# Two edits to an fp32 encoder kernel: low parts of early FFN weights by adding DMAs, and the order of the first norm

## The chip, the cores and the metric

The kernel runs on one core of a Trainium2 chip. The metric is the device time of one execution in microseconds (us); lower is better. The core's engines are named as in the profile: PE multiplies matrices (PEld is its weight load), DVE, ACT and POOL work on vectors, SP issues DMAs. POOL and ACT can issue DMAs as well. Each engine works through its own list of instructions in order, and waits at an instruction until what it needs is there.

## The reference

Two layers of an encoder over 512 tokens of width 1024, in float32. What matters here:

```python
for l in range(DEPTH):                      # DEPTH = 2
    h = rms_norm(x, g_pre_mix[l])
    z = h @ w_in[l]                         # q, k, v, conv parts, two gates
    ...                                     # windowed attention and a short convolution
    mix = (sigmoid(ga) * y_attn + sigmoid(gb) * y_conv) @ w_out[l]
    x = x + rms_norm(mix, g_post_mix[l])
    h = rms_norm(x, g_pre_ffn[l])
    f = (silu(h @ w_gate[l]) * (h @ w_up[l])) @ w_down[l]   # d_ff = 2816
    x = x + rms_norm(f, g_post_ffn[l])
```

`rms_norm(x, g)` is x / sqrt(mean(x²) + 1e-6) * g per token.

## The kernel before

**Split products.** Every float32 operand is held as two parts in a short matmul type: the high part `h` is a cast by ACT (L130 for weights, L212 for activations), the low part `lo` is raw − h, a subtraction on DVE (L131, L213). A product is then three matmuls (`mm3`, L181 to L183). There is a second way to make the low part, `split_by_dma` (L133 to L137): ACT casts (L135), ACT writes the cast's source with its sign turned into the place of `lo` (L136), and a DMA that POOL issues adds the source to it (L137), which leaves what the rounding of −src lost. As the lines stand:

```python
nc.scalar.copy(h, src)
nc.scalar.activation(lo, src, AF.Copy, scale=-1.0)
nc.gpsimd.dma_start(out=lo.bitcast(F32), in_=src, accum_op=ALU.add)
```

Weights come as 512 KB tiles: `raw` (3 buffers) or `u` (`unit`); split halves lie in `hl` tiles (8 buffers), 256 KB a part.

**FFN pairs.** The 22 gate/up pairs of a layer are computed by a scheme with seven products instead of eight (class `Pair`), numbered 1 to 7; (0,6) below means product 6 of pair 0. Products 2, 1 and 4 take a raw block of weights as it stands, products 5, 6, 3 and 7 take sums of blocks, made by DVE (L438). `need` loads, `prep` splits, `product` multiplies; `run_pairs` walks over a fixed list `seq`, and ahead of product n it loads for the next 10 products, and splits for the next 5. Where a product is in the pair's `by_dma`, its split is done up to 10 products ahead, by `split_by_dma`. The two gates of the mixer are pairs of the same class (`Gates`), with `by_dma = (4,)`; the FFN's pairs have none. `seq` begins with products 2 and 1 of the first five pairs (`EARLY`), then (0,5), (1,5), (0,6) and so on.

**The right-hand operands** of the FFN (class `Rights`) are sums of blocks of the normed activations. `turn(t)` transposes one token tile of 128 tokens on PE (L372) and makes what can be made from it; `sums(2)`, `sums(3)` make the rest once tiles 2 and 3 are there.

**The tail of w_out.** `down` multiplies by w_out; its last five k are kept and done tile by tile, so that the four token tiles end one after the other. Ahead of that, `ahead()` issues the loads of the first FFN weights and splits products 2 and 1 of pairs 0 to 2 (six splits). For each token tile, `post_norm` takes two square sums on ACT (L234), forms v on DVE, r on POOL (L228), and scales; `pre_norm` does the same once more for the FFN's norm. `turn(0)` stands after half of tile 2, `turn(1)` after half of tile 3; `turn(2)` and `turn(3)` among the first FFN products.

**The first norm** (layer 0, L608 and on) is written in a fixed order for all engines: loads, square sum, scaling, split of the first weights, transposes, products.

The rest is put in order by a scheduler, engine by engine, when the kernel is built.

Of the kernel before, what the change touches and what calls it, by code (L numbers as in the profile page):

```python
# [16 lines left out]
P = 128  # L17
D = 1024
# [10 lines left out]
FT = DFF // P  # L29
EPS = 1e-6  # L30
AHEAD = 5
LEAD = 12
NEG = -1e30
THETA = 500000.0
# [33 lines left out]
def encoder(ctx: ExitStack, tc: tile.TileContext, a, out):  # L68
    nc = tc.nc
# [9 lines left out]
    def in_order(*engines):  # L79
        return tc.manual_schedule(engines=set(engines))  # L80
# [3 lines left out]
    def nm(s):  # L84
        names[s] = names.get(s, -1) + 1
        return f"{s}_{names[s]}"

    def bank():
        return pp.tile([P, 512], F32, tag="bank", name=nm("bank"))
# [4 lines left out]
    def t4(shape, dtype=F32):  # L94
        return sp.tile(shape, dtype, tag="t4", bufs=6, name=nm("t4"))

    def t2(shape, dtype=F32):
        return sp.tile(shape, dtype, tag="t2", bufs=6, name=nm("t2"))

    def small(n, s="sm"):  # L100
        return sp.tile([P, n], F32, tag=s, bufs=4, name=nm(s))


    ident = cp.tile([P, P], F32, name="ident")
# [10 lines left out]
    def load_constants():  # L115
        nc.sync.dma_start(tab, a["tab"])
        nc.sync.dma_start(sink, a["attn_sink"].rearrange("l h -> (l h)").partition_broadcast(P))
        nc.sync.dma_start(cw_rows, a["conv_w"].rearrange("l j (c p) -> (l j c) p", p=P))
# [23 lines left out]
    def load_cols(w, c0, n, k0=0):  # L142

        raw = raw_tile()
        k = 1024 // n
        nc.sync.dma_start(
            raw.rearrange("p (k c) -> p k c", k=k),
            w[k0 * P : (k0 + k) * P, c0 : c0 + n].rearrange("(k p) c -> p k c", p=P),
        )
        return raw  # L150
# [4 lines left out]
    def split_cols(raw, n):  # L155

        tiles = []
        for hf in range(2):
            hl = hl_tile()
            split_w(raw[:, hf * 512 : hf * 512 + 512], hl[:, 0], hl[:, 1])  # L160
            tiles.append(hl.rearrange("p a (k c) -> p a k c", c=n))
        per = 512 // n
        return lambda part, k: tiles[k // per][:, part, k % per]

    def w_cols(w, c0):
        return split_cols(load_cols(w, c0, P), P)
# [53 lines left out]
    def rstd(ss):  # L220

        v = small(1, "v")
        nc.vector.tensor_scalar(v, ss, EPS, None, op0=ALU.add)
        return inv_sqrt(v)

    def inv_sqrt(v):
        r = small(1, "r")
        nc.gpsimd.tensor_tensor(out=r, in0=v, in1=half, op=ALU.pow)  # L228
        return r

    def square_sum(src, n):
        junk = t2([P, n], BF16)
        s = small(1, "ss")
        nc.scalar.activation(junk, src, AF.Square, scale=1.0 / 32.0, accum_out=s)  # L234
        return s

    def scale_rows(x, r, g):
        nc.vector.scalar_tensor_tensor(x, x, r, g, op0=ALU.mult, op1=ALU.mult)
# [5 lines left out]
    def turn(t, xs, hT):  # L244

        ts = slice(t * P, (t + 1) * P)
        for hf in range(2):
            pt = bank()
            for j in range(4):
                nc.tensor.transpose(  # L250
                    pt[:, j * P : (j + 1) * P], xs[:, (4 * hf + j) * P : (4 * hf + j + 1) * P], ident
                )
            ks = slice(4 * hf, 4 * hf + 4)
            split_to(hT[:, 0, ks, ts], hT[:, 1, ks, ts], pt.rearrange("p (k c) -> p k c", k=4))
# [247 lines left out]
    EARLY = 5  # L502
    READY = 3

    def orders(n, early):

        after = {1: 2, 6: 1, 7: 6, 4: 7, 3: 5}
        seq, at, opened = [], {}, 0

        def free(i, p):  # L510
            before = after.get(p)
            if before is None:
                return True
            if (i, before) not in at:
                return False
            return p == 1 or len(seq) - at[i, before] >= 3

        for i in range(early):
            seq += [(i, 2), (i, 1)]
            at[i, 2], at[i, 1] = len(seq) - 2, len(seq) - 1  # L520
        for i in range(2):
            at[i, 5] = len(seq)
            seq.append((i, 5))
        opened = early
        while len(seq) < 7 * n:
            left = [i for i in range(opened) if (i, 4) not in at]
            pick = next(
                ((i, p) for i in left for p in (5, 6, 3, 7, 4) if (i, p) not in at and free(i, p) and (p != 4 or (i, 3) in at)), None
            )
            if opened < n and (len(left) < 2 or pick is None):  # L530
                for p in (2, 1):
                    at[opened, p] = len(seq)
                    seq.append((opened, p))
                opened += 1
                continue
            if pick is None:
                pick = next((i, p) for i in left for p in (5, 6, 3, 7, 4) if (i, p) not in at)
            at[pick] = len(seq)
            seq.append(pick)
        return seq  # L540

    def run_pairs(pairs, seq, before=lambda n: None):
        for n, (i, p) in enumerate(seq):
            before(n)
            for j, q in seq[n : n + 2 * AHEAD]:
                pairs[j].need(q)
                if q in pairs[j].by_dma:
                    pairs[j].prep(q)
            for j, q in seq[n : n + AHEAD]:
                pairs[j].prep(q)  # L550
            pairs[i].product(p)
# [3 lines left out]
    g = t4([P, D])  # L555
    normed = [t4([P, D]) for _ in range(NT)]
    xsrc = a["x"]

    seq, gate_seq = orders(FT, EARLY), orders(KT, 2)

    for l in range(DEPTH):
# [44 lines left out]

        if l == 0:
            with in_order(E.PE, E.Activation, E.DVE, E.Pool, E.SP):  # L608
                nc.scalar.dma_start(g, a["g_pre_mix"][0].partition_broadcast(P))
                raws = []  # L610
                for t in range(NT):
                    nc.sync.dma_start(normed[t], a["x"][t * P : (t + 1) * P, :])
                    if t < 3:
                        raws.append(load_cols(w_in, *((V0, KV * HD, t * KT // 2) if t < 2 else (K0, P))))
                scale_rows(normed[0], rstd(square_sum(normed[0], D)), g)
                hv = [split_cols(raws[0], KV * HD)]
                r1 = rstd(square_sum(normed[1], D))
                turn(0, normed[0], hT)
                raws.append(load_cols(w_in, K0 + P, P))
                load_constants()  # L620
                scale_rows(normed[1], r1, g)
                hv.append(split_cols(raws[1], KV * HD))
                value_product(0, range(KT // 2))
                r2 = rstd(square_sum(normed[2], D))
                turn(1, normed[1], hT)
                value_product(0, range(KT // 2, KT))
                scale_rows(normed[2], r2, g)
                hk = [split_cols(raws[2], P)]
                value_product(1)
                value_split(0)  # L630
                scale_rows(normed[3], rstd(square_sum(normed[3], D)), g)
                hk.append(split_cols(raws[3], P))
                ka = [bank(), bank()]
                gemm_half(ka[:1], hk[:1], xs, 0)
                turn(2, normed[2], hT)
                value_split(1)
                gemm_half(ka[1:], hk[1:], xs, 0)
                turn(3, normed[3], hT)
                value_product(2)
                value_product(3)  # L640
                value_split(2)
                value_split(3)
            taps()
        else:
            hv = [split_cols(load_cols(w_in, V0, KV * HD, i * KT // 2), KV * HD) for i in range(2)]
            hk = [w_cols(w_in, K0 + i * P) for i in range(2)]
            value_tile(0)
            value_tile(1)
            turn(2, normed[2], hT)
            ka = [bank(), bank()]  # L650
            gemm_half(ka[:1], hk[:1], xs, 0)
            value_tile(2)
            turn(3, normed[3], hT)
            gemm_half(ka[1:], hk[1:], xs, 0)
            value_tile(3)
# [173 lines left out]
        total, done = (KT - 2 + 4 * KT) * KT, 0  # L829
        for _ in range(LEAD):  # L830
            next(steps)
        total -= LEAD
        for i, piece in enumerate(pieces):
# [74 lines left out]
        pairs = []  # L908
        for f in range(FT):
            pairs.append(Gated(r, a["w_gate"][l], f * P, a["w_up"][l], f * P))  # L910
            pairs[f].f = f

        def ahead():
            for i in range(READY):
# [31 lines left out]
        normed = [None] * NT  # L946
# [53 lines left out]
```

## Time and profile before

| | |
|---|---|
| time, median of 3 runs | 1663.45 us (1663.43 to 1664.44) |
| profiled execution | 1662.62 us, of it 1660.8 us in the profile's span |
| granted clock of PE, mean | 0.998 |
| stages of layer 0 (us of the span) | first norm 0 to 16; tail of w_out about 447 to 484; FFN start about 484 to 520 |
| FFN start of layer 1 | about 1305 to 1344 |
| adding DMAs in all | 16, from 360.8 to 1243.5 us |

The instructions of one line are a group; a row of the timeline has the start, the duration, the engine, the line, what was written from what, and in square brackets how long the engine had been idle and what ended that. A row of the waits has the total, the number and the longest. "q0 software_dynamic" is the queue of the DMAs that POOL issues, "q1 hardware_dynamic" that of SP and ACT. Lines are those of this kernel; the changed kernel's are 1 to 11 higher (1 higher up to L543).

### The profile page before, as it was taken

Reading aid. Unit: us, or ns where it says so; the run is one execution under the profiler, and the core shown is the slowest. Engines: PE = TensorE matmul, PEld = TensorE weight load, DVE = VectorE, ACT = ScalarE, POOL = GpSimd, SP = SyncE. Lnnn points to the kernel's source line nnn. Section 1 sums busy time; section 2 is a strip of 40 time slices with the busy share of each in tenths; the row PEclk is TensorE's granted clock in tenths of the full one; section 3 lists DMA queues with packets and bytes.
Section 4 is the critical chain, followed back from the end, with each engine's and each line's share of the span. In section 5 each row is a group of like instructions: output and inputs, shape, how many; then the busy total and the mean of one; then the engine's idle time right before and its main releaser. Section 6 shows DMA issues by size and latency. Waiting matters only on the chain.

```text
span 1660.8 us, 26449 instructions
## 1 busy us (share of the span) xinstructions
PE 1636.2 (99%) x10033; PEld 1470.2 (89%) x10033; DVE 1237.5 (75%) x2398; ACT 929.5 (56%) x1958; POOL 86.2 (5%) x130
## 2 busy tenths in 40 slices
PE   7999999999999999999999999999999999999998
PEld 7888888889989999988898888888998899999886
DVE  6988876749779988854469788756696898888442
ACT  5666666547656555543346676564575565556331
POOL 0000000000011100000000000000010011001000
PEclk9999999999999999999999999999999999999999
DMA  6322222345652333343413222223457243343332
GB/s 203 95 77 77 64 83 70 89 115 127 183 160 77 102 102 105 116 136 134 148 61 102 76 77 77 77 77 97 101 156 204 92 112 94 104 112 121 108 114 76
DMA packets 249248, 178.63 MB, mean 108 GB/s; under 512 B 5744, under 2 KB 233120, under 8 KB 249120
## 3 DMA queue, kind: packets, MB, share of 16 engines
q1 hardware_dynamic: 246096, 171.18, 35.1%
q0 software_dynamic: 2304, 4.20, 1.6%
q8 instruction: 78, 1.28, 0.3%
q10 hardware_dynamic: 720, 1.57, 0.3%
q14 instruction: 50, 0.41, 0.1%
HBM read 164.34 MB, written 8.39 MB: 104 GB/s over the span
## 4 chain that ended last, share of the span: by engine, by line
PE 96%; DVE 2%; DMA 1%; ACT 1%; issue 0%; POOL 0%; POOLq 0%; DVEq 0%; SPq 0%; ACTq 0%
PE bank L182 30%; PE bank L183 29%; PE bank L181 29%; PE bank L690 2%; PE bank L737 2%; PE bank L724 2%; PE bank L250 0%; DVE u L213 0%; DMA u<-in_w_up_dram 0%; DVE h L213 0%; DMA t<-in_x_dram 0%; ACT t L234 0%; DVE t L438 0%; DVE hl L131 0%; PE bank L372 0%
## 5 line engine op out<-in xcount | busy, mean ns | idle before, releaser
L181 PE MATMUL bank<-h,hl 128*128 128x256 f32 (+1 forms) x1536 | 493.7, 321 | 1.4 <-DVE h L213 1.4
L182 PE MATMUL bank<-h,hl 128*128 128x256 f32 (+1 forms) x1536 | 490.4, 319 | 0.4 <-DVE hl L131 0.4
L183 PE MATMUL bank<-h,hl 128*128 128x256 f32 (+1 forms) x1536 | 490.1, 319 | 0.0
L131 DVE TENSOR_TENSOR hl<-raw,hl 128x512 fp32r<-128x512 f32 x396 | 269.9, 692 | 167.6 <-ACT hl L130 166.2
L130 ACT CAST hl<-raw 128x512 fp32r<-128x512 f32 x396 | 241.8, 620 | 258.8 <-PE bank L183 216.7
L183 PEld LDWEIGHTS bank<-h,hl 128*128 128x128 f32 x1536 | 292.7, 191 | 20.8
L181 PEld LDWEIGHTS bank<-h,hl 128*128 128x128 f32 x1536 | 292.9, 191 | 19.9 <-DVE h L213 2.2
L181 PE MATMUL bank<-u,hl 128*128 128x256 f32 (+1 forms) x976 | 305.6, 313 | 4.1 <-DVE u L213 3.4
L182 PEld LDWEIGHTS bank<-h,hl 128*128 128x128 f32 x1536 | 292.9, 191 | 18.1 <-DVE hl L131 0.6
L182 PE MATMUL bank<-u,hl 128*128 128x256 f32 (+1 forms) x976 | 304.7, 312 | 2.9 <-ACT u L212 1.8
L183 PE MATMUL bank<-u,hl 128*128 128x256 f32 (+1 forms) x976 | 304.1, 312 | 0.0
L181 PEld LDWEIGHTS bank<-u,hl 128*128 128x128 f32 x976 | 186.6, 191 | 15.3 <-DVE u L213 3.8
L182 PEld LDWEIGHTS bank<-u,hl 128*128 128x128 f32 x976 | 186.8, 191 | 13.4 <-ACT u L212 2.2
L183 PEld LDWEIGHTS bank<-u,hl 128*128 128x128 f32 x976 | 186.8, 191 | 10.2
L131 DVE TENSOR_TENSOR hl<-t,hl 128x512 fp32r<-128x512 f32 x240 | 176.9, 745 | 22.5 <-ACT hl L130 19.9
L130 ACT CAST hl<-t 128x512 fp32r<-128x512 f32 x240 | 147.6, 621 | 72.4 <-DVE t L438 47.0
L182 PE MATMUL bank<-hl,u 128*128 128x512 f32 x304 | 118.3, 389 | 0.0
L181 PE MATMUL bank<-hl,u 128*128 128x512 f32 x304 | 118.3, 389 | 0.0
L183 PE MATMUL bank<-hl,u 128*128 128x512 f32 x304 | 118.3, 389 | 0.0
L710 ACT ACTIVATE t<-t,neg 128x256 f32<-128x256 f32 (+1 forms) x128 | 70.4, 552 | 21.1 <-DVE neg L705 20.8
L438 DVE TENSOR_TENSOR t<-t,raw 128x512 f32<-128x512 f32 x112 | 76.7, 696 | 1.2
L906 POOL TENSOR_TENSOR u<-t 128x256 f32<-128x256 f32 x44 | 51.8, 1178 | 398.0 <-DVE t L492 196.9
(137 smaller groups left out, 2275.1 us busy)
## 6 DMA issues: line engine op xcount, KB each, us to landing
raw<-in_w_in_dram SPq DMA_DIRECT2D x88, 512.0 KB, 3.9
u<-in_w_up_dram SPq DMA_DIRECT2D x44, 512.0 KB, 6.1
raw<-in_w_down_dram SPq DMA_DIRECT2D x44, 512.0 KB, 3.5
raw<-in_w_gate_dram SPq DMA_DIRECT2D x40, 512.0 KB, 3.9
raw<-in_w_conv_proj_dram SPq DMA_DIRECT2D x16, 512.0 KB, 4.3
raw<-in_w_attn_proj_dram SPq DMA_DIRECT2D x16, 512.0 KB, 4.3
u<-in_w_in_dram SPq DMA_DIRECT2D x16, 512.0 KB, 5.5
raw<-in_w_out_dram SPq DMA_DIRECT2D x16, 512.0 KB, 3.6
```

Source lines behind the costliest of these rows:

```text
L130: nc.scalar.copy(h, raw)
L131: eng.tensor_tensor(out=lo, in0=raw, in1=h.bitcast(F32), op=ALU.subtract)
L181: nc.tensor.matmul(acc, wh, xl, start=first, stop=False, skip_group_check=goes_on)
L182: nc.tensor.matmul(acc, wl, xh, start=False, stop=False, skip_group_check=goes_on)
L183: nc.tensor.matmul(acc, wh, xh, start=False, stop=last, skip_group_check=goes_on)
L438: add = lambda out, x, y: nc.vector.tensor_tensor(out=out, in0=x, in1=y, op=ALU.add)
L690: nc.tensor.matmul(s[:, :w], q, kk[g][:, 1 - part, lo_b * P : lo_b * P + w], start=part == 0, stop=part == 1)
L710: nc.scalar.activation(p, p, AF.Exp, bias=neg[:, i : i + 1], accum_out=den[:, i : i + 1])
L724: nc.tensor.transpose(pt[:, i * P : (i + 1) * P], p[:, n * P : (n + 1) * P], ident)
L737: nc.tensor.matmul(o, v, hl[:, 1 - part], start=n == 0 and part == 0, stop=kb == hi_b and part == 1)
L906: nc.gpsimd.tensor_tensor(out=out[:, TH:], in0=self.v[:, 1], in1=self.out0[:, TH:], op=ALU.mult)
```

## The change

1. **FFN.** Pairs 0 to 4 of both layers get `by_dma = (2, 1, 4)`: 15 low parts per layer, 30 in all, are made by an activation on ACT and an adding DMA instead of a subtraction on DVE.
2. **Look-ahead.** Splits by DMA are done up to 8 products ahead instead of 10 (`FAR`), for the mixer's gates too.
3. **First norm.** The load of `g_pre_mix` goes from ACT's queue to SP's, behind the first x tile. PE does 30 transposes of the identity, whose result nothing reads, at the start. The first token tile is scaled in two halves.

```diff
+FAR = 8
...
             for j, q in seq[n : n + 2 * AHEAD]:
                 pairs[j].need(q)
+            for j, q in seq[n : n + FAR]:
                 if q in pairs[j].by_dma:
                     pairs[j].prep(q)
...
-                nc.scalar.dma_start(g, a["g_pre_mix"][0].partition_broadcast(P))
+                idle = bank()
+                for _ in range(30):
+                    nc.tensor.transpose(idle[:, :P], ident, ident)
                 raws = []
                 for t in range(NT):
                     nc.sync.dma_start(normed[t], a["x"][t * P : (t + 1) * P, :])
+                    if t == 0:
+                        nc.sync.dma_start(g, a["g_pre_mix"][0].partition_broadcast(P))
...
-                scale_rows(normed[0], rstd(square_sum(normed[0], D)), g)
+                r0 = rstd(square_sum(normed[0], D))
+                for c in (slice(0, 512), slice(512, D)):
+                    scale_rows(normed[0][:, c], r0, g[:, c])
...
             pairs[f].f = f
+            if f < EARLY:
+                pairs[f].by_dma = (2, 1, 4)
```

What this does to the order on ACT, in the tail of w_out of layer 0. Before, after the last split of pair 2 (`raw_4725`), the two square sums of token tile 0 (`t_96`, `t_97`) and the one of its pre norm (`t_98`) follow each other:

```order
L130 CAST hl_4747<-raw_4725 128x512
L130 CAST hl_4750<-raw_4725 128x512
L234 ACTIVATE t_96_4788,ss_4789<-bank_4577 128x512
L234 ACTIVATE t_97_4795,ss_4796<-bank_4578 128x512
L234 ACTIVATE t_98_4805,ss_4806<-t_93_4783 128x1024
```

Now each split has a second row (L137), and the splits of pair 3 (`u_61` holds its gate weights) stand between the square sums:

```order
L136 CAST hl_4787<-raw_4757 128x512
L137 ACTIVATE hl_4787<-raw_4757 128x512
L235 ACTIVATE t_96_4826,ss_4827<-bank_4609 128x512
L136 CAST hl_5065<-u_61_4761 128x512
L137 ACTIVATE hl_5065<-u_61_4761 128x512
L136 CAST hl_5069<-u_61_4761 128x512
L137 ACTIVATE hl_5069<-u_61_4761 128x512
L235 ACTIVATE t_97_4833,ss_4834<-bank_4610 128x512
```

The second square sum `t_97` moved behind four operations on `u_61`.

On POOL, the last gate's adding DMA was followed at once by the r of the first post norm:

```order
L137 DMA hl_4401<-u_46_4307 128x512
L228 TENSOR_TENSOR r_4799<-v_4792,half 128x1
L228 TENSOR_TENSOR r_4810<-v_4808,half 128x1
```

Now the adding DMAs of pairs 0 to 3 stand ahead of it (the last four of eight are shown):

```order
L138 DMA hl_4783<-raw_4757 128x512
L138 DMA hl_4787<-raw_4757 128x512
L138 DMA hl_5065<-u_61_4761 128x512
L138 DMA hl_5069<-u_61_4761 128x512
L229 TENSOR_TENSOR r_4837<-v_4830,half 128x1
```

Eight DMAs moved in front of the first r; the two of pair 4 stand behind the eighth r.

On DVE, at the FFN start of layer 0, the subtractions of pairs 3 and 4 (`u_61`, `u_62`) stood behind the last pre norm's scaling (L242), among the pairs' outputs (L483):

```order
L242 SCALAR_TENSOR_TENSOR t_100_4998<-t_99_4997,r_5024,t_92_4575 128x1024
L131 TENSOR_TENSOR hl_5060<-t_108_5057,hl_5060 128x512
L483 TENSOR_TENSOR t_101_5063<-bank_5027,t_101_5063 128x256
L131 TENSOR_TENSOR hl_5078<-u_61_4729,hl_5078 128x512
L131 TENSOR_TENSOR hl_5094<-u_61_4729,hl_5094 128x512
L483 TENSOR_TENSOR t_102_5097<-bank_5081,t_102_5097 128x256
L131 TENSOR_TENSOR hl_5112<-u_62_4731,hl_5112 128x512
L131 TENSOR_TENSOR hl_5128<-u_62_4731,hl_5128 128x512
```

Now they are gone, and the sums for the right-hand operands (L400, L403, L214) follow sooner:

```order
L243 SCALAR_TENSOR_TENSOR t_100_5036<-t_99_5035,r_5062,t_92_4607 128x1024
L132 TENSOR_TENSOR hl_5106<-t_108_5103,hl_5106 128x512
L484 TENSOR_TENSOR t_101_5113<-bank_5073,t_101_5113 128x256
L439 TENSOR_TENSOR t_110_5201<-u_63_4765 128x512
L214 TENSOR_TENSOR h_4604<-u_66_5096,h_4604 128x4x128
L484 TENSOR_TENSOR t_102_5145<-bank_5132,t_102_5145 128x256
L132 TENSOR_TENSOR hl_5204<-t_110_5201,hl_5204 128x512
L400 SCALAR_TENSOR_TENSOR u_66_5096<-u_66_5096,u_64_4936 128x4x128
```

Four rows left this stretch, and L400 of the third token tile, which came after the fourth tile's first rows, moved up to here.

## The prediction

> **What bounds the kernel now.** I read the page first, then the waits of PE, then timelines where those waits lie.
>
> ```profile
> PE 1636.2 (99%) x10033; PEld 1470.2 (89%) x10033; DVE 1237.5 (75%) x2398; ACT 929.5 (56%) x1958; POOL 86.2 (5%) x130
> ...
> PE bank L250 <- DVE t L238: 9.5, 1, 9.5
> PE bank L181 <- DVE u L213: 3.4, 2, 1.7
> PE bank L182 <- ACT u L212: 1.8, 2, 0.9
> PE bank L182 <- DVE hl L131: 1.5, 4, 0.5
> ```
>
> PE is busy 99% of the span. The waits that it has (columns: total, times, longest; the four largest are shown, and sum to 16 us) lie at the start, 9.5, and where the FFN of each of the two layers begins. So the change can win only in these two places, and wherever it makes PE wait anew it costs one for one. The first norm:
>
> ```profile
> 6.12 1.06 ACT L234 ACTIVATE t<-t 128x1024 bf16<-128x1024 f32 x1 [3.65 <-DMA t<-in_x_dram]
> 8.12 1.29 DVE L238 SCALAR_TENSOR_TENSOR t<-t,r,t 128x1024 f32<-128x1024 f32 x1 [0.67 <-POOL r L228]
> 9.29 1.06 ACT L234 ACTIVATE t<-t 128x1024 bf16<-128x1024 f32 x1 [0.16 <-DMA t<-in_x_dram]
> 9.46 1.97 PE L250 MATMUL bank<-ident,t 128*128 128x128 f32 x8 [9.46 <-DVE t L238]
> 10.62 0.58 ACT L212 CAST h<-bank 128x512 fp32r<-128x512 f32 x1 [0.18 <-PE bank L250]
> 12.36 0.41 PE L183 MATMUL bank<-hl,h 128*128 128x256 f32 x1
> 12.57 0.41 PE L181 MATMUL bank<-hl,h 128*128 128x256 f32 x1
> 12.70 1.27 DVE L238 SCALAR_TENSOR_TENSOR t<-t,r,t 128x1024 f32<-128x1024 f32 x1
> ```
>
> The x tile sets the first square sum, and everything to the first product hangs on it. Matmuls follow each other here at 0.21 us (12.36, 12.57). The FFN start of layer 0, and as windows of both layers (columns: length, busy of PE, PEld, DVE, ACT, POOL, granted clock, DMA share, GB/s):
>
> ```profile
> 500.00:512.00 12.00, 9.40 (x64) 8.95 (x63) 12.00 (x22) 6.98 (x14) 0.00 (x0) 0.86 0.06 15
> 512.00:524.00 12.00, 11.54 (x96) 11.34 (x95) 11.81 (x22) 7.70 (x14) 1.80 (x2) 1.00 0.70 187
> 1320.00:1332.00 12.00, 8.70 (x64) 7.72 (x64) 12.00 (x21) 7.49 (x15) 0.00 (x0) 1.00 0.02 6
> ...
> 492.17 1.28 DVE L131 TENSOR_TENSOR hl<-u,hl 128x512 fp32r<-128x512 f32 x2
> 493.71 1.28 DVE L131 TENSOR_TENSOR hl<-u,hl 128x512 fp32r<-128x512 f32 x2
> 505.59 0.38 PE L181 MATMUL bank<-u,hl 128*128 128x256 f32 x1 [1.68 <-DVE u L213]
> 506.05 0.68 DVE L131 TENSOR_TENSOR hl<-t,hl 128x512 fp32r<-128x512 f32 x1
> 517.08 0.68 DVE L131 TENSOR_TENSOR hl<-u,hl 128x512 fp32r<-128x512 f32 x1
> 517.82 0.39 PE L182 MATMUL bank<-u,hl 128*128 128x256 f32 x1 [0.46 <-DVE hl L131]
> ```
>
> DVE is busy for all 12.00 us of the second stage in both layers, while PE stands idle for 2.6 and 3.3 us of it: DVE is the bound there. One DVE operation follows the other at 0.60 us (two end to end take 1.28 at 492.17, one takes 0.68 at 506.05).
>
> **The change, part by part.**
>
> *Gain at the FFN start.* The change takes 15 subtractions per layer from DVE. Six lie in the tail of w_out, where DVE is no bound (below). Four are the rows at 492.17 and 493.71 (2.4 us at 0.60), one the row at 517.08, which is the lo of pair 0's product 4 and holds PE back last. I moved the DVE rows forward by these steps, in the new order. The operand of pair 0's product 6 is then ready at 504.2 and not 505.5, and DVE holds PE for the last time at pair 1's product 6, whose lo is done at 508.7. From there PE has 61 matmuls to the end of pair 0's product 4, at 0.12 us (11.54 us for 96 in the window 512 to 524): 516.0. Before, that product ended about 1.4 us after the row at 517.82, at 519.2. Gain: 3.2 us per layer. Bounds: DVE loses five steps ahead of that point, 3.0 us, and layer 0 can also win back the half clock (0.86 of 12 us, 1.7 us): at most 4.7. New waits of some 2.0 us remain in my replay; set against the idle time of layer 1 (3.3 + 0.46), at least 1.8.
>
> *What the adding DMAs cost in the tail of w_out.* Three kinds of row: the instructions, the tail, the DMA engines.
>
> ```profile
> L137 POOL DMA_DIRECT2D hl<-u x16 | 14.0, 873 | 367.6 <-PE bank L183 283.0 <-DVE t L856 42.9 <-ACT hl L136 32.8
> L136 ACT ACTIVATE hl<-u 128x512 fp32r<-128x512 f32 x16 | 10.1, 633 | 0.0
> ...
> 453.43 1.14 ACT L130 CAST hl<-raw 128x512 fp32r<-128x512 f32 x2 [0.59 <-DMA raw<-in_w_gate_dram]
> 459.37 1.14 ACT L130 CAST hl<-raw 128x512 fp32r<-128x512 f32 x2 [2.49 <-DMA raw<-in_w_gate_dram]
> 461.58 0.60 ACT L234 ACTIVATE t<-bank 128x512 bf16<-128x512 f32 x1 [0.49 <-PE bank L183]
> 462.55 0.56 POOL L228 TENSOR_TENSOR r<-v,half 128x1 f32<-128x1 f32 x1 [38.84 <-DVE v L266]
> 469.40 0.55 POOL L228 TENSOR_TENSOR r<-v,half 128x1 f32<-128x1 f32 x1 [2.96 <-DVE v L266]
> 477.13 0.55 POOL L228 TENSOR_TENSOR r<-v,half 128x1 f32<-128x1 f32 x1 [3.77 <-DVE v L266]
> 484.64 0.39 PE L181 MATMUL bank<-h,hl 128*128 128x256 f32 x1 [0.87 <-DVE h L213]
> 484.83 0.55 POOL L228 TENSOR_TENSOR r<-v,half 128x1 f32<-128x1 f32 x1 [3.42 <-DVE v L266]
> ```
>
> Each lo by DMA costs ACT one more activation (0.63 us) and POOL one issue (0.87). In the new order ACT does, between the two square sums of the first token tile, the casts and negations of pair 3's gate weights: four operations, 2.2 us (two casts take 1.14, so some 0.55 each), and they wait for that load. The second square sum (461.58) stands behind them, and behind it DVE's v, POOL's r and the whole post norm; on POOL the r stands behind the eight DMAs too. So whatever delays that load by D delays the norm. Call the delay of the row at 461.58 D0.
>
> How long? That load was issued at 454.08 and landed 6.9 us later, at 461.0. Rows of the DMA engines (share over 100% is full; one adding DMA alone; one beside a load; the loads of this tail; a load that met an adding DMA and one that didn't):
>
> ```profile
> q0 software_dynamic: 67, 0.14, 117.1%
> ...
> q0 software_dynamic: 78, 0.16, 93.1%
> q1 hardware_dynamic: 102, 0.05, 23.8%
> ...
> q1 hardware_dynamic: 6044, 3.31, 118.6%
> ...
> u<-in_w_gate_dram SPq DMA_DIRECT2D x1, 512.0 KB, 6.9
> ...
> raw<-in_w_in_dram SPq DMA_DIRECT2D x1, 512.0 KB, 5.3
> ...
> raw<-in_w_in_dram SPq DMA_DIRECT2D x1, 512.0 KB, 3.9
> ```
>
> An adding DMA of 256 KB moves 67 packets in a us with all engines full; it has 144 (2304 for 16), so it holds them for about 2 us. Beside a load its packets and the load's alternate (78 to 102), which all but stops a load: the loads alone move 6044 in 11 us, some 550 a us. The load that met one took 1.4 us more (5.3 against 3.9). The tail's loads already fill the engines for 11 us (118.6%). Six adding DMAs issue between 454.6 and 462, and four to six meet or precede the load in question: 4 x 1.4 = 5.6 to 6 x 2.0 = 12 us. It lands at 466.6 to 473 instead of 461.0. I take 469, five or six at 1.4, the price of the pair of rows nearest to this case. The square sum then starts at 469 + 2.2 = 471.2: D0 = 9.6 (range 7.2 to 12.6). Without any contention D0 isn't zero: the raw tile of 459.37 takes four operations and not two, to 461.5, the first square sum goes to 462.1 and the four of pair 3 to 464.3: D0 = 2.7.
>
> What reaches PE: tile by tile the first r's stand 6.85, 7.73 and 7.70 us apart. The first gap is the chain's own pace (nothing waits for PE there), the others that of PE; so a late chain wins back 0.88 + 0.85 = 1.7 us, and pair 0's product 2 (484.64), whose h waits for the second tile's turn behind this chain, is late by D0 − 1.7: 7.9 us. Net per layer 7.9 − 3.2 = 4.7 us slower. The break-even is D0 = 4.9.
>
> *Later by-DMA preps.* The lo's of pair 4 stand on POOL behind the eight r's. They land, by the row below, 4.8 us after their issue, some 1.6 us before PE wants them by my replay; at 7.3 they would cost 1 to 2 us, which I leave to the range. The look-ahead cut from ten to eight products also moves the gates' product 4: PE has no wait in that stage, where a product is twelve matmuls at 0.12, 1.4 us, and the landing takes 4.8. Price nothing; cover: eight products, 11 us.
>
> ```profile
> DMA to landing us min/median/max: 3.3/4.8/7.3
> ```
>
> *First norm.* The x tile and g were issued together and shared the engines; with g behind x, x lands an estimated 1.4 us earlier (g's 512 KB at the tail's 300 GB/s is 1.7), and the half-row scaling lets the first transposes start 0.6 earlier still: about 7.5 instead of 9.46. But ACT works in order: the square of the second tile, whose x lands no earlier (9.29, to 10.44 with its readout), stands ahead of the cast at 10.62. So that cast gains only 0.2 us. What else: the idle transposes, 30 at 0.16 to 0.25 us (1.97 for 8), run from 1.3 to 6.1 or 8.7, before the old 9.46 in any case, so they hold up nothing, and may bring the full clock: twelve matmuls at 0.12 instead of 0.21, 1.1 us, of which DVE's second scaling (12.70, by its input 0.44 earlier at most) lets through part. Gain 0.2 to 1.2 us. Between the idle transposes' and first transposes' end and the first product PE is idle for about 2.6 us. By the nearest row, the wait of 1.68 us at 505.59, after which the window's clock was 0.86, the gain is 0.3. The Trainium skill (TensorE: Matmul & The Clock Gate, Part 1) says that the throttle returns only after at least one idle window of about 3.4 us, which a gap of 2.6 would not fill: by that the gain is 1.0. The trace is divided on it: layer 0's wait of 1.68 was followed by 0.86, layer 1's, no shorter, by 1.00. I take 0.7, the middle of 0.2 and 1.2.
>
> *Sum.* 2 x 4.7 − 0.7 = +8.7 us. On the profiled execution (1662.62, span 1660.8 and 1.8 around it) that is 1671.3; on the median of the runs, 1663.45, it is 1672.
>
> **Rivals.**
>
> B, faster: the adding DMAs do not hold up pair 3's load by more than about one of them (it lands by 463). Then D0 is 2.7 to 3.6, PE late by 1.0 to 1.9, the gain 3.2: 2 x (−2.2 to −1.3) − 0.7 = −5.1 to −3.3, with the larger gains down to −7, so 1656.5 to 1660. For it: the tail's loads have up to 7 us from issue to landing, part of it queueing behind each other, and work queued for later may give way. Against it: packets alternate wherever both queues have work. It decides at D0 = 4.9 per layer, a landing at 463.7.
>
> C, no change: fair shares, D0 3.6 to 6.9, gain and cost cancel within 3.3 us. That is 0.2%, about what a measurement of this kernel tells from no change. Also here: DVE turns out to be bound in the FFN start by the transposes of the last token tile, so that neither gain nor much cost shows.
>
> D, the half clock after the new waits: PE stalls of 3 to 8 us in the tail, and each may be followed by a window like that of 0.86, up to 1.7 us. For it speaks the row at 505.59, against it layer 1's 1.00. With one such window in each layer the forecast becomes 1675.5; it is a part of the forecast's case, a quarter of its chance.
>
> **How the numbers follow.** The forecast's case, D0 7 to 12.6, with D in it (0.14 of 0.55), gives 2 x (2.1 to 7.7) − 0.7 = +3.5 to +14.7, 1667 to 1678, a us more with D: chance 0.55, all slower. B 0.31, all faster. C 0.14. Cases of both signs hold much, so the range reaches over all: 1656.5 to 1679; the forecast's own is 1667 to 1679.
>
> **What would show it.** In the trace after: ACT idle ahead of pair 3's casts for the DMA of w_gate, the second square sum of the first token tile at 466 to 474 and not 461.6; a new PE wait at the turns (L373) for the pre norm's DVE row, twice, 3 to 8 us; the software queue's packets up from 2304 by 30 x 144 to 6624. For the gain: the waits for u L214 and ACT u L213 at the FFN start go or shrink below 1 us, and the last one (hl L132 at pair 0's product 4) goes. First norm: transposes at about 7.5, first product still near 11.0. I am wrong if pair 3's load lands by 463, or if the norm's rows on ACT do not wait for it.

## The result, and the profile after

| | before | changed |
|---|---|---|
| median of all runs so far | 1663.27 us (6 runs, 1662.53 to 1664.44) | 1673.97 us (6 runs, 1672.41 to 1675.13) |
| profiled span | 1660.8 us | 1672.4 us |
| ratio, 95% interval | | 1.0063 (1.005 to 1.0076) |

The change makes the kernel 10.7 us slower; the forecast was 1672, in a range from 1656.5 to 1679 that held both signs. The page and PE's waits after (total, times, longest):

```profile
PE 1643.8 (98%) x10063; PEld 1477.0 (88%) x10063; DVE 1219.0 (73%) x2369; ACT 942.1 (56%) x1988; POOL 105.2 (6%) x160
...
q0 software_dynamic: 6624, 12.06, 4.2%
...
PE bank L182 <- DVE h L214: 7.7, 2, 4.7
PE bank L373 <- DVE v L264: 3.2, 2, 2.5
PE bank L183 <- DMA hl<-u: 2.6, 3, 1.3
PE bank L182 <- ACT h L213: 2.3, 1, 2.3
PE bank L183 <- DVE hl L132: 2.1, 4, 0.7
PE bank L182 <- DVE t L493: 1.4, 2, 0.7
```

The 9.5 us at the start are gone from the list (PE has the idle transposes there), the waits for u L213 have shrunk, and in their place PE waits 7.7 us for h (pair 0's product 2 behind a late post norm), 3.2 us at the turns, and 2.6 us for adding DMAs themselves.

**Where the time went.** The start of every PE matmul can be set beside that of the same matmul before (the n-th of the one trace against the n-th of the other, the idle ones left out). The difference is a staircase:

| at | lag behind before, us |
|---|---|
| first transposes | −2.0 |
| from 17 us of the span to the tail of w_out, layer 0 | +0.06 |
| after turn(0), layer 0 | +2.7 |
| after pair 0's product 2, layer 0 | +4.9, then +6.45 with a half clock |
| end of the FFN start, layer 0 | +4.96 |
| from 684 us | +6.9 |
| after pair 0's product 2, layer 1 | +12.0, then +13.35 with a half clock |
| at (0,6), layer 1 | +10.9 |
| end of the FFN start, layer 1 | +12.0 |
| from 1510 us | +11.2 |

So each layer loses 6.4 to 6.5 us in the tail of w_out and wins back 1.3 to 1.5 at the FFN start; the front gives nothing. The steps between (+1.9 by 684 us, −0.9 at 1510) are late loads of the FFNs, far from the change (last section).

**Layer 0's tail.** ACT, POOL and PE, each from its own timeline:

```profile
461.45 0.57 ACT L235 ACTIVATE t<-bank 128x512 bf16<-128x512 f32 x1
465.63 0.62 ACT L136 CAST hl<-u 128x512 fp32r<-128x512 f32 x1 [3.52 <-DMA u<-in_w_gate_dram]
467.20 0.63 ACT L137 ACTIVATE hl<-u 128x512 fp32r<-128x512 f32 x1
467.73 0.57 ACT L235 ACTIVATE t<-bank 128x512 bf16<-128x512 f32 x1
...
468.69 0.89 POOL L229 TENSOR_TENSOR r<-v,half 128x1 f32<-128x1 f32 x1
...
474.27 1.09 PE L373 MATMUL bank<-ident,t 128*128 128x128 f32 x8 [2.48 <-DVE v L264]
489.54 0.39 PE L182 MATMUL bank<-h,hl 128*128 128x256 f32 x1 [3.03 <-DVE h L214]
```

ACT sits idle for 3.52 us, in front of pair 3's casts, for the load of w_gate. The second square sum comes at 467.73 and not 461.58: D0 = 6.15. PE pays at the first turn and at product 2.

**Layer 1's tail** is another story. ACT again, then SP's issue of the second token tile's x, DVE's wait for it, and PE:

```profile
1288.64 0.61 ACT L136 CAST hl<-u 128x512 fp32r<-128x512 f32 x1
1290.72 0.58 ACT L235 ACTIVATE t<-bank 128x512 bf16<-128x512 f32 x1
1304.35 1.06 ACT L235 ACTIVATE t<-t 128x1024 bf16<-128x1024 f32 x1 [7.75 <-DVE t L271]
...
1285.85 10.60 SPq L893 DMA_DIRECT2D t<-xd  x1
1302.97 1.29 DVE L271 SCALAR_TENSOR_TENSOR t<-t,r,t 128x1024 f32<-128x1024 f32 x1 [4.44 <-DMA t<-xd]
...
1316.88 0.58 PE L182 MATMUL bank<-h,hl 128*128 128x256 f32 x1 [4.65 <-DVE h L214]
```

Pair 3's casts wait for nothing here, and the second square sum (1290.72, less the 6.9 us by which the layer began late) is only 1.6 us behind before's 1282.21. What is late is the second token tile's x: DVE's L271 needs it, and ACT waits 7.75 us for that. The DMA issues of these four us (KB, us from issue to landing; 2 and 4 of a kind as medians):

```profile
u<-in_w_gate_dram SPq DMA_DIRECT2D x2, 512.0 KB, 12.2
hl<-raw POOLq DMA_DIRECT2D x4, 256.0 KB, 7.5
u<-in_w_up_dram SPq DMA_DIRECT2D x1, 512.0 KB, 17.5
t<-xd SPq DMA_DIRECT2D x1, 512.0 KB, 17.0
```

This x took 17.0 us; before, the same load took 6.5 (7.1 in layer 0). Its issue alone held SP for 10.60 us; before, 1.67.

**The FFN start.** The waits that are left there:

```profile
510.70 0.39 PE L182 MATMUL bank<-u,hl 128*128 128x256 f32 x1 [0.34 <-DVE u L214]
515.25 0.39 PE L183 MATMUL bank<-u,hl 128*128 128x256 f32 x1 [0.71 <-DVE hl L132]
521.10 0.39 PE L183 MATMUL bank<-u,hl 128*128 128x256 f32 x1 [1.27 <-DMA hl<-u]
1352.88 0.39 PE L183 MATMUL bank<-u,hl 128*128 128x256 f32 x1 [0.98 <-DMA hl<-u]
```

The 1.68 has become 0.34, as DVE is relieved; but product 4's low parts, now by DMA, are the last to come.

**The first norm**, with the windows from 9 to 21 us (the seventh number is the granted clock):

```profile
4.40 1.06 ACT L235 ACTIVATE t<-t 128x1024 bf16<-128x1024 f32 x1 [2.38 <-DMA t<-in_x_dram]
7.45 1.32 PE L251 MATMUL bank<-ident,t 128*128 128x128 f32 x8 [0.41 <-DVE t L239]
9.39 1.06 ACT L235 ACTIVATE t<-t 128x1024 bf16<-128x1024 f32 x1
10.44 1.05 ACT L213 CAST h<-bank 128x512 fp32r<-128x512 f32 x2
11.06 0.38 PE L182 MATMUL bank<-hl,h 128*128 128x256 f32 x1 [2.29 <-ACT h L213]
...
9.00:15.00 6.00, 3.60 (x19) 3.32 (x20) 4.95 (x9) 4.70 (x10) 0.68 (x2) 0.81 1.10 352
15.00:21.00 6.00, 6.00 (x48) 6.00 (x47) 4.82 (x8) 4.39 (x9) 0.96 (x2) 0.91 0.94 275
```

The x tile lands 1.7 us earlier and the transposes start 2.0 earlier, but the cast behind ACT's square of the second tile starts 0.2 earlier; after the gap of 2.29 us the mean clock of the window is 0.81. The same window reads 1.00 in the kernel before, but that is no full clock: its clock record begins at 15.01 us, and its matmuls up to there stand 0.21 us apart (rows in the prediction). So the idle transposes did bring the clock up, at 5.9 us of the span, and the gap gave it back: the matmuls stand 0.12 us apart from 12.0 to 12.7, and 0.21 again from 12.7 to 16.1.

### The profile page after: what moved, and what is told of

Its sections match the earlier page's. It is cut to its first block, busy times and chain, and to the rows that moved or that the text cites. A ratio compares the mean times of both kernels' runs of the same rounds, so it can differ in the third digit from the quotient of the medians.

```text
span 1672.4 us, 26620 instructions
## 1 busy us (share of the span) xinstructions
PE 1643.8 (98%) x10063; PEld 1477.0 (88%) x10063; DVE 1219.0 (73%) x2369; ACT 942.1 (56%) x1988; POOL 105.2 (6%) x160
## 3 DMA queue, kind: packets, MB, share of 16 engines
q0 software_dynamic: 6624, 12.06, 4.2%
## 5 line engine op out<-in xcount | busy, mean ns | idle before, releaser
L131 ACT CAST hl<-raw 128x512 fp32r<-128x512 f32 x384 | 235.2, 620 | 255.3 <-PE bank L184 222.1
L132 DVE TENSOR_TENSOR hl<-raw,hl 128x512 fp32r<-128x512 f32 x384 | 261.6, 692 | 159.0 <-ACT hl L131 157.6
L132 DVE TENSOR_TENSOR hl<-t,hl 128x512 fp32r<-128x512 f32 x240 | 180.7, 759 | 22.5 <-ACT hl L131 20.6
L704 DVE CUSTOM_DVE_ANT_0 t<-bank,tab,sink 128x256 f32<-128x256 f32 (+1 forms) x128 | 65.7, 542 | 6.1 <-PE bank L699 5.9
```

What stands on the lines that cost most here:

```text
L131: nc.scalar.copy(h, raw)
L132: eng.tensor_tensor(out=lo, in0=raw, in1=h.bitcast(F32), op=ALU.subtract)
L704: nc.vector.tensor_tensor_reduce(out=p, in0=s[:, :w], in1=mask[:, m0 : m0 + w], scale=HD**-0.5, scalar=sink[:, h : h + 1], op0=ALU.add, op ...
```

## The experiments

Diffs are against the kernel before, unless they say otherwise. "The FFN edit" is parts 1 and 2 of the change.

**1. The two halves of the change apart.** The front alone is part 3 of the change, the FFN alone parts 1 and 2.

> Only the edits of the first norm (g behind the first x tile, 30 idle transposes, scaling by halves); no adding DMAs in the FFN. My theory: the front neither wins nor loses; in the changed kernel's trace PE's first transposes start 2.0 us earlier, but by the end of the second token tile's transposes PE is at +0.06 us against before. So within 0.1 % of before, and PE 0.0 to 0.1 us late from 17 us of the span on. Rival: the front does carry part of the 10.7 us through what follows it (the throttle); then this kernel is over 2 us slower.

> Only the FFN edit (by_dma = (2, 1, 4) for pairs 0 to 4, look-ahead 8); the first norm as before. My theory: the whole of the change's time is here, +10 to +11.5 us (1673 to 1675), with pair 3's gate weights landing 4 to 5 us late in layer 0 and the second token tile's x late in layer 1. Rival (the front carries part): clearly under +9.

Front alone: 1663.32 us against 1663.08, ratio 1.0004 (0.9995 to 1.0013). FFN alone: 1674.06, ratio 1.0067 (1.0054 to 1.0079). The whole loss is the FFN edit's. PE of the front alone was some 0.1 us ahead until 615 us; by 679 it was 1.4 us behind, which it lost far from the front, to late loads (last section). One part of the second expectation failed: in the trace of the FFN alone the layers have changed places. In layer 0 pair 3's weights landed in 6.5 us, and x was late (ACT idle for 8.77 us, tail 8.2 us longer); in layer 1 the weights were late (12.4 us, ACT idle for 4.13 us, tail 6.1 us longer).

**2. No adding DMAs in the tail, same order on ACT.** The FFN edit, with this in place of its last lines:

```diff
+            if f < EARLY:
+                pairs[f].by_dma = (2, 1, 4) if f >= READY else (4,)
```

> Products 2 and 1 of pairs 0 to 2 are split on DVE again, so no adding DMA issues before the loads of pair 3 and of the second token tile's x have landed; pairs 3 and 4 keep (2, 1, 4), pairs 0 to 2 keep (4). The order on ACT is as in the changed kernel: pair 3's four operations stand between the square sums. My theory (the adding DMAs hold up the loads): pair 3's gate weights land at about 461 as before, the square sum behind them is late by 1.7 us only, which the slack takes; the FFN start wins 1.5 to 2.4 us per layer: -2 to -5 us against before. Rival (what costs is the order on ACT and POOL, not the DMA engines): still +3 us or more per layer, so +6 to +10.

1660.91 us against 1663.08, ratio 0.9989 (0.9981 to 0.9998): the loss is gone, though pair 3's four operations stand between the square sums as in the changed kernel:

```profile
459.45 0.19 ACT L235 ACTIVATION_READ_ACCUMULATOR t<-bank 128x1 f32 x1
459.67 0.62 ACT L136 CAST hl<-u 128x512 fp32r<-128x512 f32 x1
461.77 0.57 ACT L235 ACTIVATE t<-bank 128x512 bf16<-128x512 f32 x1
```

The load is there in time, the square sum comes at 461.77. So the splits by adding DMA of pairs 0 to 2 are what costs, and the order on ACT only carries it. (This edit also takes six activations from ACT and six issues from POOL in each tail; experiment 5 keeps both, at 0.55 us an issue in place of 0.87.) PE's lag at the FFN start of layer 0 goes from −0.75 to −2.2, and in layer 1 from −1.25 to −2.9. PE waits there for product 4's adding DMAs:

```profile
PE bank L183 <- DMA hl<-u: 2.2, 4, 0.8
```

**3. The adding DMAs kept, the order on ACT mended.** The FFN edit with a look-ahead of 6 puts pair 3's splits behind the post norm:

```diff
-FAR = 8
+FAR = 6
```

> As the FFN edit alone, but with a look-ahead of 6 products: pair 3's splits then stand behind the post norm on ACT and POOL, while the six adding DMAs of pairs 0 to 2 still issue in the tail. My theory: the loads starve all the same, and the second token tile's x (needed at about 470 in layer 0) becomes the late one in both layers: layer 0 loses 1 to 4 us instead of 4.9, layer 1 about 5 as before: +5 to +9 us. Rival (the order on ACT is all that costs): the loss goes, -2 to -5 us as in the kernel without tail adds.

1680.03 us, ratio 1.010 (1.0086 to 1.0114): worse, which neither theory expected. The tail did as mine said: layer 0 loses 2.8 us at product 2, for x. ACT in layer 0, and PE's wait for adding DMAs:

```profile
461.26 0.60 ACT L235 ACTIVATE t<-bank 128x512 bf16<-128x512 f32 x1
474.60 1.06 ACT L235 ACTIVATE t<-t 128x1024 bf16<-128x1024 f32 x1 [5.79 <-DVE t L271]
...
PE bank L183 <- DMA hl<-u: 9.8, 7, 3.8
```

The square sum is on time, and the second tile's x is late (5.79 us of idle ACT). The rest, which I had not priced, is the FFN start: with a shorter look-ahead the low parts of products 2, 1 and 4 land after PE wants them, 9.8 us in seven waits. Product 4's DMAs took 4.6 to 7.4 us here, and so need their look-ahead.

**4. Product 4: by DVE, or by DMA but sooner.** Against the kernel of 2, first product 4 is taken out of `by_dma`, then it is left in and looked up to 10 products ahead.

```diff
-            if f < EARLY:
-                pairs[f].by_dma = (2, 1, 4) if f >= READY else (4,)
+            if READY <= f < EARLY:
+                pairs[f].by_dma = (2, 1)
```
```diff
-            for j, q in seq[n : n + FAR]:
-                if q in pairs[j].by_dma:
+            for d, (j, q) in enumerate(seq[n : n + 2 * AHEAD]):
+                if q in pairs[j].by_dma and (d < FAR or q == 4):
                     pairs[j].prep(q)
```

> Only products 2 and 1 of pairs 3 and 4 are split by adding DMAs; product 4 of the FFN pairs is split on DVE again, so nothing at the FFN start waits for an adding DMA's landing. My theory: the 2.2 us that PE waited for hl<-u in the kernel without tail adds go, but DVE does the two subtractions of product 4 again and holds PE there for 0.5 us or so as before the change: -2 to -4 us against before. Rival (the late product 4 costs nothing, since DVE is as late): the same as the kernel without tail adds, -2.2, and PE waits for hl L132 in place of the DMA.

> As the kernel without tail adds, but product 4 is split up to 10 products ahead instead of 8, so its two adding DMAs at the FFN start issue about two products (2.9 us) sooner and ahead of the loads that fill the DMA engines from 507 us. My theory (the gain falls short of the forecast because product 4's low part lands late): the waits of PE for hl<-u go, -4 to -5 us against before. Rival (DVE sets the end there anyway): no more than the -2.2 of the kernel without tail adds.

By DVE: 1657.7 against 1662.89, ratio 0.997 (0.9959 to 0.9981). By DMA, sooner: 1658.34, ratio 0.9973 (0.9962 to 0.9984). In both, PE waits for no adding DMA any more. Their first rows of PE's waits past the start, the one with product 4 by DVE first:

```profile
PE bank L182 <- DVE h L214: 2.1, 2, 1.3
PE bank L183 <- DVE hl L132: 1.9, 6, 0.5
```
```profile
PE bank L183 <- DVE hl L132: 2.1, 4, 0.7
PE bank L182 <- DVE h L214: 1.9, 2, 1.1
```

From pair 0's product 2 to the end of the FFN start, PE gains 2.5 us in each layer with product 4 on DVE, and 3.1 and 3.2 (layers 0 and 1) with it on time by DMA. The forecast's 3.2 is there once the DMA is not late. With 2.2 us of DMA waits, the kernel of experiment 2 kept half of it (1.4 and 1.6).

**5. What in an adding DMA holds up the loads.** The six DMAs of the tail copy without adding: first their own source, then the sine table (mostly zeros). Against the FFN alone:

```diff
-        nc.gpsimd.dma_start(out=lo.bitcast(F32), in_=src, accum_op=ALU.add)
+        if plain:                                   # products 2 and 1 of pairs 0 to 2
+            nc.gpsimd.dma_start(out=lo.bitcast(F32), in_=src)   # second run: in_=sin
+        else:
+            nc.gpsimd.dma_start(out=lo.bitcast(F32), in_=src, accum_op=ALU.add)
```

> As the FFN edit alone, but the six DMAs of products 2 and 1 of pairs 0 to 2 copy the source instead of adding it (so the low parts of these products are not what they should be; order, sizes and queue are the same). Theory a (the engine time of adding is what starves the loads): a copy is done faster than an adding DMA's 2.0 us per 256 KB, pair 3's weights and the second token tile's x land 2 to 5 us sooner than with adding, and the loss is 3 to 8 us instead of 11. Theory b (what POOL's queue carries goes ahead of the loads whatever it is): the loss stays at 10 to 12 us.

> As the kernel with plain copies for the six DMAs of pairs 0 to 2 (256 KB each, POOL's queue, no adding), but the copies take their data from the sine table, which is mostly zeros, so that the low parts of these products are not what they should be. It is to give a trace of the tail. Theory a (adding is what takes the DMA engines' time): each copy holds the engines for about 1 us and not 2, pair 3's weights land within 2 us of before (461) in layer 0, and the loss is 4 to 8 us. Theory b (POOL's queue goes ahead whatever it carries, and takes as long): landing at 465 to 466 as in the changed kernel, loss 10 to 12.

Copies of the source: 1670.03 us against 1662.89, ratio 1.0031 (1.0022 to 1.004). Its trace is of an execution of 7004 us, with matmuls of 1.0 us each, which the ratio leaves out and from which nothing of the tail can be read; hence the second run: 1666.43 against 1663.05, ratio 1.0023 (1.0013 to 1.0033). By these ratios a third to a half of the loss stays, against 1.0067 with adding; the second run's 3.4 us is a little under what theory a gave it. The DMA queues from 457 to 465 us, with adding (the changed kernel), then copying:

```profile
q0 software_dynamic: 494, 0.91, 62.6%
q1 hardware_dynamic: 2315, 1.16, 52.0%
```
```profile
q1 hardware_dynamic: 2487, 1.25, 60.4%
q0 software_dynamic: 417, 1.39, 50.5%
```

In the same 8 us POOL's queue moves 0.91 MB in 62.6% of the engines' time with adding, and 1.39 MB in 50.5% as copies: with the shares taken of 8 us, 5.5 us per MB against 2.9 (two adding DMAs of pair 3 are still among the second). Adding costs the engines about twice a copy. But the loads run at half their rate in both (1.16 and 1.25 MB; before, 3.31 MB in 11 us, so 2.4 in 8): theory a holds for the size, b for the fact that POOL's DMAs, of whatever kind, are served beside loads queued before them. Pair 3's weights show the same in layer 1, where their issue ended 1.0 us after POOL's first DMA began: 9.1 us to landing with copies, 11.6 to 12.5 with adding in like cases (table of experiment 6), 7.3 before. Their landing in layer 0, at 459.9, decides nothing: an issue as early as that one landed in time with adding too.

**6. The x ahead of the FFN weights.** The FFN alone, with the second token tile's x loaded among w_out's weights:

```diff
+        x1 = t4([P, D])
+        nc.sync.dma_start(x1, src[P : 2 * P, :])
...
+            if t == 1:
+                x, f = x1, t4([P, D])
+            else:
+                x, f = t4([P, D]), t4([P, D])
+                nc.sync.dma_start(x, src[t * P : (t + 1) * P, :])
```

> As the FFN edit alone, but the second token tile's x is loaded ahead of the FFN weights, so that it can't starve behind the adding DMAs. My theory: in layer 1, where pair 3's weights landed in time and only this x was late (the ACT engine sat idle 7.8 us for the scaling that needs it), the loss of 5 us becomes a gain of 1 to 2; layer 0, where pair 3's weights were late by 4.6 us, keeps 3 to 5: in all +2 to +5 us against before. Rival (the x is not what PE waits for): +10 to +11 as with the FFN edit alone.

1669.57 us against 1663.05, ratio 1.0047 (1.0031 to 1.0062): 4.5 us better than the FFN alone, but +6.5 and not the +2 to +5 that I expected. The expectation took the layers from the changed kernel; here they stand as in the FFN alone. Layer 0, where x was the late load, loses 2.4 us in its tail and not 8.2, and ends 1.0 us behind where it was; layer 1, where pair 3's weights are late in both (12.5 us to landing here), loses 5.9 us in its tail and not 6.1, and ends 4.3 us further behind. So x is a victim of its own, and with it out of the way pair 3's weights are left; which layer has them late is not fixed. Side by side, over the four kernels with six adding DMAs in the tail (SP's issue of pair 3's gate weights ends so many us after POOL's first adding DMA begins its issue; us to landing):

| kernel, layer | issue ends, us after | to landing, us |
|---|---|---|
| changed, layer 1 | 0.0 | 6.5 |
| FFN alone, layer 0 | 0.1 | 6.5 |
| look-ahead 6, layer 0 | 0.6 | 8.0 |
| x early, layer 0 | 0.7 | 8.1 |
| FFN alone, layer 1 | 0.9 | 12.4 |
| look-ahead 6, layer 1 | 1.1 | 11.6 |
| changed, layer 0 | 1.3 | 11.8 |
| x early, layer 1 | 1.4 | 12.5 |

A load whose issue ends within 0.1 us of the start of POOL's first takes 6.5 us, no longer than before the change (6.9 and 7.3); at 0.6 to 0.7 us it takes 8, and from 0.9 us on some 5 us more. This is a pattern in eight cases, not an experiment on the issue time. Everything behind it (pair 4's weights, 14.7 to 18.8 us in all eight) lands 0.1 to 0.7 us after the last of the adding DMAs then under way; after the first two or three these land some 1.6 us apart.

**7. The front's gap filled.** The front alone, and 13 more idle transposes between the transposes of the first tile and the first product:

```diff
                 turn(0, normed[0], hT)
+                for _ in range(13):
+                    nc.tensor.transpose(idle[:, :P], ident, ident)
```

> Only the front edits, and 13 more idle transposes on PE behind the transposes of the first token tile, which fill the 2.3 us before the first product. My theory (the throttle comes back in that gap, and takes the 0.9 us that the front had won by 14 us): granted clock 1.00 and not 0.81 from 9 to 15 us, and PE 0.4 to 1.0 us ahead of before from 17 us on. Rival (the gap is too short to matter; the clock falls for another reason): clock still about 0.8 and PE at +0.06 us as with the front alone.

The windows from 9 to 15 us, of the front alone and of the front filled:

```profile
9.00:15.00 6.00, 3.53 (x16) 3.33 (x17) 5.01 (x9) 4.49 (x9) 0.61 (x2) 0.72 1.10 352
```
```profile
9.00:15.00 6.00, 4.46 (x35) 3.82 (x34) 5.15 (x9) 5.15 (x11) 0.55 (x1) 1.00 1.10 353
```

The clock stays at 1.00 instead of 0.72, and PE is 0.9 us ahead of before up to 677 us. In the times it doesn't show: 1662.8 against 1662.89, ratio 1.0 (0.9992 to 1.0009). In the trace the 0.9 was lost again where DVE waits for a late load in the FFNs (PE idle for 0.58 us at 677 and 0.94 at 1479; last section).

**8. Both gains together**: products 2 and 1 of pairs 3 and 4 alone by DMA, and the filled front.

> The two gains together: only products 2 and 1 of pairs 3 and 4 by adding DMAs, and the first norm with the gap filled by 13 more idle transposes. If they add: -5.2 - 0.7 = -5.9 us against before (1657), within 1 us. Rival (the front's gain is lost later, as in every timed run of it so far): -5.2.

1657.93 us against 1663.05, ratio 0.9968 (0.9955 to 0.998). That is the same as without the front (0.997). The fastest versions are this one and the two of experiment 4, and between them nothing can be told; the kernel of experiment 2 is faster than before too, by 2.2 us.

## Why the prediction was right, and where its steps were off

- **The place and the carrier**: right for layer 0. The rows foreseen are there: ACT idle ahead of pair 3's casts, the square sum inside 466 to 474, PE late at L373 and at product 2, 6624 packets. The waits at L373 were 2.48 and 0.74 us, not 3 to 8.
- **How far the load is pushed**: too far. I had it land at 469 behind five or six adding DMAs at 1.4 us; it landed at 465.6, behind three that landed ahead of it. D0 was 6.15 and not 9.6, below my range of 7.2 to 12.6. Two figures there don't follow from my own sum (landing + 2.2 − 461.58): the range's upper end should be 13.6, and the break-even landing 464.3, not 463.7. Neither moves the forecast.
- **D0 − 1.7 for product 2**: 4.45 by the measured D0, 4.9 measured. That step holds.
- **The half clock after the new waits** (rival D): it came, in both layers, 1.4 to 1.6 us each. I had given it a quarter of the forecast's chance.
- **Layer 1**: wrong victim. I made layer 1 a copy of layer 0; there the load of pair 3 was issued in time, D0 was 1.6, and the x behind it starved. By D0 alone that layer would have gained. The rule "the loads issued behind POOL's first adding DMA are late by 5 to 9 us; which of them is wanted first?" would have covered both.
- **The gain at the FFN start**: 3.2 forecast, 1.3 to 1.5 measured. The replay of DVE was right: experiment 4 shows 3.1 and 3.2, and in experiment 2, whose PE is 0.75 us ahead there, the two waits for DVE end at 503.50 and 508.05, so 504.25 and 508.8 by the before's times, where I had 504.2 and 508.7. The step that failed is the one that called product 4's low part on time. I took 4.8 us to landing; pair 0's took 5.67 in layer 0 and pair 1's 8.0, and PE waited 1.27 us at 521.10, and 0.36 and 0.98 in layer 1.
- **The front**: +0.06 instead of −0.7. The transposes, the cast at 10.44 and the first product at 11.06 came as worked out. I took the middle between clock kept and clock lost; the row with the lost clock was the one to take. The Trainium skill's rule (TensorE: Matmul & The Clock Gate, Part 1) that it takes an idle window of some 3.4 us does not agree with this place: 2.29 us of idle and a wait of 0.34 were followed by a window clock of 0.81, and with the gap filled it stayed at 1.00.
- **The sum was nearer than its terms, and that is luck.** Product 2 was late by 4.8 and 5.1 us in the two layers, where I had 7.9; a half clock that the sum left out made that 6.4 and 6.5; and of the gain of 3.2 only 1.5 and 1.3 came. Net 4.9 and 5.2 us against 4.7. The front's missing 0.7 and 1 us net of late loads in the FFNs, which no term had, make up the rest (forecast +8.7; +11.2 at the end of this trace, +10.7 by the medians).
- **Rival B** (the load not held up) is about what experiment 2 makes of the kernel, without the front. Its −2.2 us is less than the −5.1 to −3.3 that the rival was given, for want of product 4's low parts on time; with product 4 out of the way it was −5.2.

## What to carry to other kernels

Work moved from a busy engine to DMAs is not free where loads fill the DMA engines: look at what is queued on the loads' side at that moment, and price every load behind, not just the next. Move only what has slack: of the 15 low parts per layer, the four of pairs 3 and 4 alone brought 5 us, with the five of product 4 it was 2, and with the six in the tail it was a loss of 11. A part made by DMA needs a look-ahead longer than its landing under load (5 to 8 us at the FFN start here), and an in-order engine should not stand behind a load that can be late while it has shorter work that others wait for.

## What the runs showed of the hardware

- A DMA from POOL's queue that starts while SP's queue is full is not served after it: the tail's adding DMAs land 1.4 to 2.6 us apart from the start, and a load whose issue ends 0.9 us or more after the first of them begins loses some 5 us (table in experiment 6). Whether this is packets taken in turn or a rank between queues is open.
- Whether PE's clock falls after an idle stretch is not settled by the stretch's length: in the changed kernel it fell after 2.29 us (0.81, shown above), 3.03 (at 489.54) and 4.65 (at 1316.88), and did not after 2.48 (at 474.27); before the change it fell after 1.68 us in one layer and not in the other. Each time it was at half for 3.41 us (12.70 to 16.12, 490.57 to 493.98 and 1316.59 to 1320.01 in the changed kernel, 506.53 to 509.94 before), beginning between 0.3 us before and 1.6 us after the end of the wait. So one fall costs at most 1.7 us; 1.4 to 1.6 were measured. Windows around 474.27, 489.54 and 1316.88:

```profile
474.00:482.00 8.00, 7.73 (x38) 6.53 (x39) 5.97 (x12) 4.31 (x10) 1.09 (x2) 1.00 0.57 171
486.00:494.00 8.00, 4.97 (x28) 4.55 (x27) 5.79 (x9) 3.20 (x8) 0.85 (x2) 0.79 0.41 140
1314.00:1322.00 8.00, 5.12 (x32) 5.13 (x33) 5.96 (x10) 3.04 (x7) 0.55 (x1) 0.79 0.27 75
```

- In the FFNs a load of w_up now and then takes 1.2 to 1.5 us more than its neighbours (6.6 to 6.8 for 5.3 to 5.4), and PE is idle for 0.6 to 1.2 us. In the changed kernel this happened twice in layer 0 (L493 at 622.9 and 684.3, behind DVE's wait for w_up), in the kernel before once in layer 1 (at 1498):

```profile
621.17 0.69 DVE L439 TENSOR_TENSOR t<-u 128x512 f32<-128x512 f32 x1 [2.73 <-DMA u<-in_w_up_dram]
622.86 0.39 PE L182 MATMUL bank<-u,hl 128*128 128x256 f32 x1 [0.70 <-DVE t L493]
```

  No adding DMA is near. It moves a single run by about as much as the front's edit is worth, and its cause is open.
